# Start addresses of weight units against the activations in a float32r two-block network on one NeuronCore

## The chip, the cores and the metric

One of the eight cores of a Trainium2 chip runs the kernel. The metric is the device time of one execution in microseconds, the median over several runs. Engines are named as in the profile: PE is the matmul engine and PEld its weight loads, DVE, ACT and POOL are the vector, scalar and GpSimd engines, SP issues most of the transfers.

## The reference

Two small networks of depth 2 follow each other on 256 tokens of width 1024, batch 1. Everything is float32.

```python
# first block, for i in 0, 1
x = layer_norm(a * x + 0.5 * swiglu(x, w1[i,0], w3[i,0], w2[i,0]))
x = layer_norm(a * x + token_mixing(x, w_in[i], ...))    # RWKV-7, gated linear attention, gated delta rule
x = layer_norm(a * x + 0.5 * swiglu(x, w1[i,1], w3[i,1], w2[i,1]))
x = layer_norm(a * x + sigmoid(x @ ple_gate[i]) * (p[i] @ ple_proj[i]))
# second block, latent stream h and context stream hc of 256 tokens each
h, hc = x, ctx_2
# layer 0: attention over both streams, gated MLP on both; layer 1: HGRN2, MLP on h
```

The feed-forward width is 2816 (22 tiles of 128). Nearly all arithmetic is a product of 256 tokens with a large weight matrix.

## The kernel before

**Weight units.** All large weights lie in DRAM as units of 128 partitions by 1024 float32 (512 KB). `unit` (L67) fetches one: `split` (L71) has SP start the transfer into `wr` (L77), ACT rounds it to float32r into `wh` (L78), and DVE writes the rest, `wr - wh`, into `wl` (L79). There are four buffers each of `wr` and `wh` and three of `wl`. Activations are held in the same way as a high part `xh` and a low part `xl` (in the feed-forward's middle `hh` and `hl`, in the mixing branches `bh` and `bl`). A product of two such numbers is three matmuls: high by high, low weight by high, high weight by low.

**Feature-major products.** `fm` (L95) makes a result with features on the partitions. The weight tile of 128 columns is the stationary operand and the activations, 256 tokens, are the moving one: L102 (`wh`, `xh`), L103 (`wl`, `xh`), L105 (`wh`, `xl`; L109 where the low parts are late). Each matmul has 256 columns and a weight load of its own. The up projections of the feed-forwards (`ffn2`, L132), part of the token mixing (`fm_tile`, L1141) and of HGRN2 (L1742, L1748) go this way. A unit feeds 24 of these matmuls for one stream of tokens. `ffn2` takes a list of streams: in layer 0 of the second block it has two, and then both use a unit one after the other, all 48 matmuls of a pair of units for the first stream, then 48 for the second.

**Token-major products.** `tm2` (L163) makes a result with tokens on the partitions: the activations are stationary, and the weights move, 512 columns (256 where the last block is cut in two) per matmul: L178 (`xh`, `wh`), L179 (`xh`, `wl`), L180 (`xl`, `wh`). The down projections, the gates, the branch projections (`proj`, L1115) and the output projections go this way.

**Order.** Each engine runs its own instructions in program order; which instruction stands where comes from tables of numbers that place side work between weight units. PE has the weight load of the next matmul run beside the matmul before it.

**Addresses.** A pool lays its tiles one behind the other in each partition's bytes. In the built program of before, every `wh` and `wl` begins 32 bytes past a multiple of 128 (38560, 42656, ... ; 54944, ...), and so do the first stream's `xh` and `xl` (67232, 75424). The second stream's (108224, 116416) begin 64 past a multiple of 128; so do all `hh`, `hl`, `bh` and `bl`. A step of k moves the weights by 512 bytes and the activations by 1024, so these remainders hold for the whole tile. The *distance* of a matmul is below: start of its moving operand less start of the stationary operand that is loaded beside it (that of the next matmul), modulo 128.

Of the kernel before, what the change touches and what calls it, by code (L numbers as in the profile page):

```python
# [10 lines left out]
F32 = mybir.dt.float32  # L11
F32R = mybir.dt.float32r
# [5 lines left out]
P = 128  # L18
# [4 lines left out]
KF = 22  # L23
# [4 lines left out]


PIECES = (slice(0, 256), slice(256, 1024))  # L30


class Core:
# [30 lines left out]
        self.dr = E(tc.tile_pool(name="dr", bufs=1, space=bass.MemoryType.DRAM))  # L64


    def unit(self, src):  # L67
        self.tick()
        return self.split(src)

    def split(self, src):  # L71
        nc = self.nc
        hi = self.wh.tile([P, 1024], F32R, tag="wh", name=self.nm("wh"))
        lo = self.wl.tile([P, 1024], F32R, tag="wl", name=self.nm("wl"))
        raw = lo.bitcast(F32)
        raw = self.wr.tile([P, 1024], F32, tag="wr", name=self.nm("wr"))
        nc.sync.dma_start(raw, src)  # L77
        on_act = nc.scalar.copy(hi, raw)  # L78
        on_dve = nc.vector.tensor_tensor(lo, raw, hi.bitcast(F32), ALU.subtract)  # L79
        if self.queue:  # L80
            for op, first in zip((on_act, on_dve), self.queue.pop(0)):
                self.behind(op, first)
        return hi, lo
# [48 lines left out]
    def ffn2(self, up, down, xs, scale, sink, aside={}):  # L132


        nc = self.nc
        with self.tc.tile_pool(name=self.nm("hp"), bufs=1, reuse_waits="tile") as hp:
            hs = []
            for i in range(len(xs)):
                hs.append((hp.tile([P, KF, T], F32R, tag=f"hh{i}", name=self.nm("hh")),
                           hp.tile([P, KF, T], F32R, tag=f"hl{i}", name=self.nm("hl"))))  # L140
            for m in range(KF):
                if m == 3:
                    self.load_later()
                if m in aside:
                    aside[m]()
                w = [self.unit(up[2 * m]), self.unit(up[2 * m + 1])]
                for (xh, xl), (hh, hl) in zip(xs, hs):
                    pa, pv = self.acc(), self.acc()
                    self.fm([pa[:, :T], pv[:, :T]], w, xh, xl, late=m == 0)
                    th = hp.tile([P, T], F32, tag="th", bufs=3, name=self.nm("th"))  # L150
                    nc.scalar.activation(th, pa[:, :T], AF.Tanh, scale=0.5)  # L151
                    g = hp.tile([P, T], F32, tag="g", bufs=3, name=self.nm("g"))
                    nc.vector.scalar_tensor_tensor(g, th, 1.0, pa[:, :T], ALU.add, ALU.mult)
                    nc.vector.scalar_tensor_tensor(g, g, 0.5 * scale, pv[:, :T], ALU.mult, ALU.mult)  # L154
                    nc.scalar.copy(hh[:, m], g)  # L155
                    nc.vector.tensor_tensor(hl[:, m], g, hh[:, m].bitcast(F32), ALU.subtract)
            self.spot("down")
            self.tm2(down, 0, 2, hs, KF, sink, cut=True)

    def tm(self, src, b0, nblk, xh, xl, nk, sink, last=6, cut=False):  # L160
        self.tm2(src, b0, nblk, [(xh, xl)], nk, lambda n, i, t, ps, *c: sink(n, t, ps, *c), last, cut=cut)

    def tm2(self, src, b0, nblk, xs, nk, sink, last=6, lead=0, cut=False):  # L163

        nc = self.nc
        w = {}

        def mm(z, k, b, first, end):  # L170
            u = b // 2
            if u not in w:
                w[u] = self.unit(src[u])
            o, i, t, c = z
            h, l = (x[:, (b % 2) * 512 + c.start:(b % 2) * 512 + c.stop] for x in w[u])
            s = slice(t * P, t * P + P)
            xh, xl = xs[i]
            nc.tensor.matmul(o, xh[:, k, s], h, start=first, stop=False)  # L178
            nc.tensor.matmul(o, xh[:, k, s], l, start=False, stop=False)  # L179
            nc.tensor.matmul(o, xl[:, k, s], h, start=False, stop=end)  # L180

        self.load_later()
        for n in range(nblk):
            it = [(self.acc(), i, t, slice(0, 512)) for i in range(len(xs)) for t in range(2)]
            if cut and n == nblk - 1:
                o, i, t, _ = it.pop()
                it += [(o[:, :256], i, t, slice(0, 256)), (self.spare()[:, :256], i, t, slice(256, 512))]
            ahead = lead if n == 0 else 0
            tail = 0 if n < nblk - 1 else min(nk - ahead, last if len(xs) == 1 else last // 2)
            seq = [(k, z) for i in (1, 0) for k in range(ahead) for z in it if z[1] == i]  # L190
            seq += [(k, z) for k in range(ahead, nk - tail) for z in it]
            for k, z in seq:
                mm(z, k, b0 + n * nk + k, k == 0, k == nk - 1)
            for z in it:
                for k in range(nk - tail, nk):
                    mm(z, k, b0 + n * nk + k, k == 0, k == nk - 1)
                o, i, t, c = z
                sink(n, i, t, o, *((c,) if cut else ()))
# [198 lines left out]
class Mix(Core):  # L397
# [35 lines left out]
    def inv16(self, stg):  # L433

        nc = self.nc
        V = nc.vector
        sel = [self.cc("sel")[:, i:i + 1] for i in range(2)]
        fl = lambda z: z.rearrange("p a h u -> p a (h u)")
        at = self.t([P, 16, 32], "iA", bufs=2)
        V.transpose(at, fl(stg))  # L440
        a = self.t([P, 16, 16], "ia")
        V.tensor_scalar_mul(a, at[:, :, 0:16], sel[0])
        V.scalar_tensor_tensor(a, at[:, :, 16:], sel[1], a, ALU.mult, ALU.add)
        x = self.t([P, 16, 16], "ix")
        nc.gpsimd.memset(x, 0.0)
        nc.gpsimd.memset(x.rearrange("p a b -> p (a b)")[:, 0:256:17], 1.0)
        pr = self.t([P, 16, 16], "ip")
        for i in range(1, 16):
            V.tensor_tensor(pr[:, :i, :i], x[:, :i, :i], a[:, i, :i].rearrange("p (s o) -> p s o", o=1).broadcast_to([P, i, i]), ALU.mult)
            V.tensor_reduce(x[:, i, :i], pr[:, :i, :i].rearrange("p s c -> p c s"), mybir.AxisListType.X, ALU.add)  # L450
        e = self.t([P, 16, 32], "iA", bufs=2)
        for h in range(2):
            nc.scalar.activation(e[:, :, 16 * h:16 * h + 16], x.rearrange("p t s -> p s t"), AF.Identity, scale=sel[h])
        o = self.t([P, 16, 2, 16], "iB")
        V.transpose(fl(o), e)
        return o
# [626 lines left out]
class Block(Mix):  # L1083
# [15 lines left out]
    def proj(self, l, n, o):  # L1099

        nc = self.nc
        first = not self.merged
        bh = self.t([P, 4, T], "bh", F32R, pool=self.late)
        bl = self.t([P, 4, T], "bl", F32R, pool=self.late)
        self.to_fm(lambda t: o[:, t], bh, bl, nk=4)

        def sink(half, t, ps):
            g = self.gt[n, half]
            nc.vector.scalar_tensor_tensor(g[:, t], g[:, t], 1.0, ps, ALU.add, ALU.mult)
            if first:  # L1110
                self.merged[half] = g
            else:
                m = self.merged[half]
                nc.gpsimd.tensor_tensor(m[:, t], m[:, t], g[:, t], ALU.add)
        self.tm(self.a["wbr"][l, n], 0, 2, bh, bl, 4, sink)  # L1115

    def rw_tile(self, i, ps, st={}):
        nc = self.nc
# [21 lines left out]

    def fm_tile(self, i):  # L1141
        p = self.acc()[:, :T]
        self.fm([p], [self.unit(self.wfm[i])], self.xh, self.xl)
        return p

    def token_mix(self, l, pool, ln):
# [121 lines left out]
    def first(self, es, ep, stop=None):  # L1268
        nc, tc, a = self.nc, self.tc, self.a
# [6 lines left out]

        def last_pool():
            self.xq = es.enter_context(tc.tile_pool(name="xq", bufs=1, reuse_waits="tile"))
            return self.xq
        self.consts()  # L1280
        self.x_load(pool())
# [46 lines left out]
class Second(Block):  # L1328
# [371 lines left out]
    def hgrn(self, h, st, xs):  # L1700
        nc, tc, a = self.nc, self.tc, self.a
        V = nc.vector
        with tc.tile_pool(name="hg", bufs=1, reuse_waits="tile") as p:
# [9 lines left out]
            m = tl([P, KD], "lm")  # L1713
# [17 lines left out]
            xh, xl = (self.xp.tile([P, KD, T], F32R, tag=f"x{c}0", name=self.nm("xo")) for c in "hl")  # L1731
# [5 lines left out]
            def gates(j):  # L1737
# [1 line left out]

                z = tl([P, 4, T], "z", bufs=2)  # L1740
                for d in range(2):
                    w = self.unit(a["whfm"][3 * j + d])  # L1742
                    ps = self.acc()
                    for i in range(2):
                        self.fm([ps[:, i * T:i * T + T]], [w], *xs[i])
                    nc.scalar.activation(z[:, d:4:2], ps.rearrange("p (i t) -> p i t", i=2), AF.Tanh, scale=0.5)
                pq = self.acc()[:, :T]
                self.fm([pq], [self.unit(a["whfm"][3 * j + 2])], *xs[0])  # L1748
                q = tl([P, T], "hq", bufs=2)
                nc.scalar.copy(q, pq)  # L1750
                g = tl([P, 4, T], "hgl")
# [342 lines left out]
```

## Time and profile before

| | |
|---|---|
| median of 3 runs | 2857.93 us (2857.44 to 2858.2) |
| the profiled execution | 2860.42 us, span 2858.6 us |
| mean granted clock of PE | 0.984 |
| PE busy | 2763.0 us, 97% |
| DVE, ACT, POOL busy | 1890.3, 1300.3, 203.1 us |
| read from HBM | 420.36 MB |

The profile comes from one execution, which took 2.5 us more than the median. PE's busy time is a union of pipelined matmuls, each of which is recorded as longer than its distance to the next, so the pace of the matmuls is read from their starts and not from their durations.

### The profile page before, as it was taken

The numbers are of one execution on the slowest core, as the hardware profiler recorded it, in microseconds if no ns is written. First come the engines' busy times: TensorE is split into PE (matmuls) and PEld (weight loads), VectorE is DVE, ScalarE is ACT, GpSimd is POOL, SyncE is SP. The second block draws the span as 40 slices with busy tenths as digits, with TensorE's granted clock in tenths as the row PEclk, the third lists the DMA queues.
The fourth block names the chain that finished last, engine by engine and source line by source line (L and its number), as shares of the span: only waits on it lengthen the run. The fifth ranks groups of instructions, "written<-read, shape, count | busy, mean of one in ns | idle before, by whom it ended". The sixth has DMA issues, their size and how long they took to land.

```text
span 2858.6 us, 47580 instructions
## 1 busy us (share of the span) xinstructions
PE 2763.0 (97%) x18676; PEld 2443.4 (85%) x18676; DVE 1890.3 (66%) x3852; ACT 1300.3 (45%) x2040; POOL 203.1 (7%) x332
## 2 busy tenths in 40 slices
PE   9999999999999999999999998999999999999998
PEld 8978887669978987887778986798999888898897
DVE  5658885876556657876777656786444327799664
ACT  4436543535434435634444534564333226565543
POOL 0000211020000001211010001200000001000000
PEclk9999999999999999999999999999999999999999
DMA  7555333465566555423366556202322433224554
GB/s 253 184 195 171 119 121 104 142 238 180 185 210 213 183 180 189 129 99 118 118 224 223 179 174 224 81 31 76 102 89 90 129 99 111 75 65 153 181 182 150
DMA packets 117008, 426.63 MB, mean 149 GB/s; under 512 B 13600, under 2 KB 14112, under 8 KB 115760
## 3 DMA queue, kind: packets, MB, share of 16 engines
q1 hardware_dynamic: 115168, 419.01, 44.2%
q0 software_dynamic: 1472, 4.51, 0.5%
q8 instruction: 147, 2.41, 0.3%
q14 instruction: 77, 0.63, 0.1%
q10 hardware_dynamic: 144, 0.07, 0.0%
HBM read 420.36 MB, written 3.18 MB: 148 GB/s over the span
## 4 chain that ended last, share of the span: by engine, by line
PE 83%; DVE 10%; ACT 3%; DMA 2%; issue 2%; POOL 0%; DVEq 0%; POOLq 0%; SPq 0%; ACTq 0%
PE ps L102 13%; PE ps L103 13%; PE ps L105 12%; PE ps L179 10%; PE ps L180 10%; PE ps L178 10%; DVE wl L79 2%; PE pc L487 2%; PE pc L1649 1%; PE pc L1395 1%; PE pt L243 1%; PE pt L1633 1%; PE pt L1836 1%; ACT wh L78 1%; DMA modd<-row 1%
## 5 line engine op out<-in xcount | busy, mean ns | idle before, releaser
L79 DVE TENSOR_TENSOR wl<-wr,wh 128x1024 fp32r<-128x1024 f32 x658 | 812.2, 1236 | 557.7 <-issue 198.1
L78 ACT CAST wh<-wr 128x1024 fp32r<-128x1024 f32 x658 | 688.4, 1049 | 647.9 <-PE ps L180 293.7
L102 PE MATMUL ps<-xh,wh 128*128 128x256 f32 x3280 | 938.1, 287 | 10.0 <-ACT wh L78 4.0
L103 PE MATMUL ps<-xh,wl 128*128 128x256 f32 x3280 | 932.0, 285 | 2.2 <-DVE wl L79 2.1
L105 PE MATMUL ps<-xl,wh 128*128 128x256 f32 x3168 | 900.5, 285 | 0.4 <-DVE xl L254 0.3
L102 PEld LDWEIGHTS ps<-xh,wh 128*128 128x128 f32 x3280 | 632.8, 193 | 20.8 <-ACT wh L78 6.1
L103 PEld LDWEIGHTS ps<-xh,wl 128*128 128x128 f32 x3280 | 632.4, 193 | 8.8 <-issue 4.2
L105 PEld LDWEIGHTS ps<-xl,wh 128*128 128x128 f32 x3168 | 607.4, 192 | 5.0 <-issue 3.4
L178 PE MATMUL ps<-wh,xh 128*128 128x512 f32 (+1 forms) x624 | 245.0, 396 | 5.3 <-ACT wh L78 2.9
L179 PE MATMUL ps<-wl,xh 128*128 128x512 f32 (+1 forms) x624 | 246.5, 395 | 0.8 <-DVE wl L79 0.7
L180 PE MATMUL ps<-wh,xl 128*128 128x512 f32 (+1 forms) x624 | 244.1, 393 | 0.0
L180 PE MATMUL ps<-wh,hl 128*128 128x512 f32 (+1 forms) x616 | 228.4, 371 | 0.0
L179 PE MATMUL ps<-wl,hh 128*128 128x512 f32 (+1 forms) x616 | 228.1, 370 | 0.0
L178 PE MATMUL ps<-wh,hh 128*128 128x512 f32 (+1 forms) x616 | 227.6, 370 | 0.0
L178 PEld LDWEIGHTS ps<-wh,xh 128*128 128x128 f32 x624 | 118.1, 190 | 35.7 <-ACT wh L78 3.4
L179 PEld LDWEIGHTS ps<-wl,xh 128*128 128x128 f32 x624 | 118.5, 190 | 25.3 <-DVE wl L79 2.7
L180 PEld LDWEIGHTS ps<-wh,xl 128*128 128x128 f32 x624 | 118.7, 190 | 22.3 <-issue 0.7
L151 ACT ACTIVATE th<-ps 128x256 f32<-128x256 f32 x154 | 59.2, 384 | 170.7 <-PE ps L105 160.3
L178 PEld LDWEIGHTS ps<-wh,hh 128*128 128x128 f32 x616 | 115.9, 188 | 22.6 <-DVE g L154 0.4
L179 PEld LDWEIGHTS ps<-wl,hh 128*128 128x128 f32 x616 | 115.7, 188 | 21.9
L180 PEld LDWEIGHTS ps<-wh,hl 128*128 128x128 f32 x616 | 115.7, 188 | 21.4
L155 ACT CAST hh<-g 128x256 fp32r<-128x256 f32 x154 | 62.6, 406 | 116.7 <-DVE g L154 116.6
(566 smaller groups left out, 3718.4 us busy)
## 6 DMA issues: line engine op xcount, KB each, us to landing
wr<-in_up SPq DMA_DIRECT2D x264, 512.0 KB, 3.4
wr<-in_down SPq DMA_DIRECT2D x132, 512.0 KB, 3.3
wr<-in_wtm SPq DMA_DIRECT2D x72, 512.0 KB, 3.3
wr<-in_wfm SPq DMA_DIRECT2D x62, 512.0 KB, 3.6
fr<-in_ada SPq DMA_DIRECT2D x23, 1024.0 KB, 5.6
wr<-in_ada SPq DMA_DIRECT2D x38, 512.0 KB, 4.2
wr<-in_wbr SPq DMA_DIRECT2D x24, 512.0 KB, 4.0
wr<-in_whfm SPq DMA_DIRECT2D x24, 512.0 KB, 3.3
```

The costliest lines, as they stand in the source:

```text
L78: on_act = nc.scalar.copy(hi, raw)
L79: on_dve = nc.vector.tensor_tensor(lo, raw, hi.bitcast(F32), ALU.subtract)
L102: nc.tensor.matmul(o, hi[:, w], xh[:, k], start=k == 0, stop=False)
L103: nc.tensor.matmul(o, lo[:, w], xh[:, k], start=False, stop=False)
L105: nc.tensor.matmul(o, hi[:, w], xl[:, k], start=False, stop=k == nk - 1)
L151: nc.scalar.activation(th, pa[:, :T], AF.Tanh, scale=0.5)
L155: nc.scalar.copy(hh[:, m], g)
L178: nc.tensor.matmul(o, xh[:, k, s], h, start=first, stop=False)
L179: nc.tensor.matmul(o, xh[:, k, s], l, start=False, stop=False)
L180: nc.tensor.matmul(o, xl[:, k, s], h, start=False, stop=end)
L243: nc.tensor.transpose(pt[:, j, t * P:t * P + P], self.cols(src(t), t, k + j), self.ident)
L487: nc.tensor.matmul(ps[:, 64 * u:64 * u + 64], lhs[:, u], rhs[:, u], start=True, stop=True)
```

## The change

Tiles `wh` and `wl` become 128 bytes longer (1056 elements), and a unit takes 1024 elements of its tile from an offset that the caller gives: 16 elements (64 bytes) for feature-major products, 8 elements (32 bytes) for the branch projections and for the down projections of the first block, none for all other token-major ones. Since nothing else is free in a partition, the tile `iA` of the delta rule's inverse goes from two buffers to one; a filler of 96 bytes begins the pool `xq`, which holds the second stream.

```diff
+ROOM, FM_AT, HID_AT = 32, 16, 8
...
-    def unit(self, src):
+    def unit(self, src, at=0):
         self.tick()
-        return self.split(src)
-
-    def split(self, src):
+        return self.split(src, at)
+
+    def split(self, src, at):
         nc = self.nc
-        hi = self.wh.tile([P, 1024], F32R, tag="wh", name=self.nm("wh"))
-        lo = self.wl.tile([P, 1024], F32R, tag="wl", name=self.nm("wl"))
-        raw = lo.bitcast(F32)
+        hi = self.wh.tile([P, 1024 + ROOM], F32R, tag="wh", name=self.nm("wh"))[:, at:at + 1024]
+        lo = self.wl.tile([P, 1024 + ROOM], F32R, tag="wl", name=self.nm("wl"))[:, at:at + 1024]
...
-                w = [self.unit(up[2 * m]), self.unit(up[2 * m + 1])]
+                w = [self.unit(up[2 * m], FM_AT), self.unit(up[2 * m + 1], FM_AT)]
...
-            self.tm2(down, 0, 2, hs, KF, sink, cut=True)
+            self.tm2(down, 0, 2, hs, KF, sink, cut=True, at=0 if self.fr is None else HID_AT)
...
-                w[u] = self.unit(src[u])
+                w[u] = self.unit(src[u], at)
...
-        at = self.t([P, 16, 32], "iA", bufs=2)
+        at = self.t([P, 16, 32], "iA")
...
-        e = self.t([P, 16, 32], "iA", bufs=2)
+        e = self.t([P, 16, 32], "iA")
...
-        self.tm(self.a["wbr"][l, n], 0, 2, bh, bl, 4, sink)
+        self.tm(self.a["wbr"][l, n], 0, 2, bh, bl, 4, sink, at=HID_AT)
...
-        self.fm([p], [self.unit(self.wfm[i])], self.xh, self.xl)
+        self.fm([p], [self.unit(self.wfm[i], FM_AT)], self.xh, self.xl)
...
             self.xq = es.enter_context(tc.tile_pool(name="xq", bufs=1, reuse_waits="tile"))
+            self.xq.tile([P, 24], F32, name="fillq")
...
-                    w = self.unit(a["whfm"][3 * j + d])
+                    w = self.unit(a["whfm"][3 * j + d], FM_AT)
```

(`self.fr` is None only in the second block; `tm` hands `at` on to `tm2`; the second use of `whfm` changes in the same way.) No instruction is added or removed, and the order on every engine is the same as before; what changes are addresses, and with them some semaphore waits of POOL, DVE and SP on earlier users of the same bytes.

The distances in the two built programs, over all pairs of matmuls of these products that follow each other (a pair is counted under the moving operand of its first):

| product, columns | distance before | distance after | pairs |
|---|---|---|---|
| feature-major, 256 | 0 | 64 | 8237 |
| feature-major, 256 | 32 | 64 | 1428 |
| token-major, 512 | 0 | 0 | 1502 |
| token-major, 512 | 96 | 0 | 1865 |
| token-major, 512 | 96 | 32 | 198 |
| token-major, 256 | 0 | 0 | 237 |
| token-major, 256 | 96 | 0 | 697 |
| token-major, 256 | 96 | 32 | 132 |

The 45 pairs left out lie at the seams between two kinds of product, or keep 96.

## Rows read from the trace of the kernel before

**Rows 1.** The page, part 1: busy time of each engine.

```profile
PE 2763.0 (97%) x18676; PEld 2443.4 (85%) x18676; DVE 1890.3 (66%) x3852; ACT 1300.3 (45%) x2040; POOL 203.1 (7%) x332
```

**Rows 2.** The page, part 4: the chain that ended last, by line.

```profile
PE ps L102 13%; PE ps L103 13%; PE ps L105 12%; PE ps L179 10%; PE ps L180 10%; PE ps L178 10%; DVE wl L79 2%; PE pc L487 2%; PE pc L1649 1%; PE pc L1395 1%; PE pt L243 1%; PE pt L1633 1%; PE pt L1836 1%; ACT wh L78 1%; DMA modd<-row 1%
```

**Rows 3.** Waits of PE: us in total, times, longest.

```profile
PE ps L102 <- ACT wh L78: 4.0, 3, 2.1
```

**Rows 4.** Windows, a first-block up projection: PE, PEld, DVE, ACT, POOL, clock, DMA, GB/s.

```profile
888.46:1011.44 122.98, 122.98 (x1028) 122.98 (x1026) 76.56 (x109) 59.90 (x87) 0.00 (x0) 1.00 0.58 185
```

**Rows 5.** Timeline of PE, two streams on one pair of units: start us, us.

```profile
2055.97 0.28 PE L102 MATMUL ps<-xh,wh 128*128 128x256 f32 x1
...
2061.72 0.28 PE L102 MATMUL ps<-xh,wh 128*128 128x256 f32 x1
...
2067.38 0.28 PE L102 MATMUL ps<-xh,wh 128*128 128x256 f32 x1
```

**Rows 6.** Groups of PE, inside the first, then the second stretch of rows 5.

```profile
L103 PE MATMUL ps<-xh,wl 128*128 128x256 f32 x17 | 4.8, 283 | 0.0
...
L105 PE MATMUL ps<-xl,wh 128*128 128x256 f32 x17 | 4.8, 281 | 0.0
L103 PE MATMUL ps<-xh,wl 128*128 128x256 f32 x17 | 4.7, 278 | 0.0
L102 PE MATMUL ps<-xh,wh 128*128 128x256 f32 x16 | 4.5, 280 | 0.0
```

**Rows 7.** Timeline and windows of PE: a gate at distance 0, 87 matmuls apart.

```profile
413.73 0.39 PE L180 MATMUL ps<-wh,xl 128*128 128x512 f32 x1
...
433.47 0.39 PE L180 MATMUL ps<-wh,xl 128*128 128x512 f32 x1
...
413.74:433.46 19.72, 19.72 (x88) 16.32 (x87) 19.07 (x63) 9.93 (x12) 6.70 (x4) 1.00 0.59 180
```

**Rows 8.** The same of a down projection at distance 96, 135 matmuls apart.

```profile
138.96 0.40 PE L178 MATMUL ps<-wh,hh 128*128 128x512 f32 x1
...
170.46 0.28 PE L178 MATMUL ps<-wh,hh 128*128 128x256 f32 x1
...
139.00:170.45 31.45, 31.45 (x137) 25.32 (x136) 15.45 (x15) 12.51 (x13) 0.00 (x0) 1.00 0.59 192
```

**Rows 9.** Timeline of PE: 256 columns at distance 96, then 0; 35 matmuls apart.

```profile
1068.95 0.28 PE L178 MATMUL ps<-wh,hh 128*128 128x256 f32 x1
...
1073.10 0.28 PE L180 MATMUL pc<-wh,hl 128*128 128x256 f32 x1
...
1501.04 0.28 PE L178 MATMUL ps<-wh,xh 128*128 128x256 f32 x1
...
1505.23 0.28 PE L180 MATMUL pc<-wh,xl 128*128 128x256 f32 x1
```

**Rows 10.** Around a matmul with no weight load beside it: groups, then PEld's timeline.

```profile
L103 PE MATMUL ps<-xh,wl 128*128 128x256 f32 x1 | 0.3, 279 | 0.0
...
323.18 0.19 PEld L103 LDWEIGHTS ps<-xh,wl 128*128 128x128 f32 x1
325.89 0.30 PEld L487 LDWEIGHTS pc<-iz,NT 128*128 128x128 f32 x2 [2.52 <-issue]
```

**Rows 11.** Timeline of PE: eight transposes; groups: one transpose's length.

```profile
603.83 1.03 PE L243 MATMUL pt<-cst,gate 128*128 128x128 f32 x8
...
L1420 PE MATMUL pt<-cst,row 128*128 128x128 f32 x1 | 0.3, 272 | 0.0
```

**Rows 12.** Groups of DVE and ACT in the stretch of rows 4; windows: the first 100 us.

```profile
L79 DVE TENSOR_TENSOR wl<-wr,wh 128x1024 fp32r<-128x1024 f32 x44 | 53.9, 1225 | 36.0 <-issue 27.6 <-PE ps L103 8.0 <-ACT wh L78 0.5
L78 ACT CAST wh<-wr 128x1024 fp32r<-128x1024 f32 x44 | 46.0, 1048 | 31.9 <-issue 28.8 <-PE ps L105 3.1
...
0.00:100.00 100.00, 92.88 (x748) 91.79 (x749) 59.99 (x90) 49.14 (x74) 1.28 (x12) 1.00 0.69 234
```

More of the change, by code (lines that the diff above doesn't have):

```diff
@@ L157, in ffn2, with tm, tm2 @@
             self.spot("down")
-            self.tm2(down, 0, 2, hs, KF, sink, cut=True)
-    def tm(self, src, b0, nblk, xh, xl, nk, sink, last=6, cut=False):
-        self.tm2(src, b0, nblk, [(xh, xl)], nk, lambda n, i, t, ps, *c: sink(n, t, ps, *c), last, cut=cut)
-    def tm2(self, src, b0, nblk, xs, nk, sink, last=6, lead=0, cut=False):
+            self.tm2(down, 0, 2, hs, KF, sink, cut=True, at=0 if self.fr is None else HID_AT)
+    def tm(self, src, b0, nblk, xh, xl, nk, sink, last=6, cut=False, at=0):
+        self.tm2(src, b0, nblk, [(xh, xl)], nk, lambda n, i, t, ps, *c: sink(n, t, ps, *c), last, cut=cut, at=at)
+    def tm2(self, src, b0, nblk, xs, nk, sink, last=6, lead=0, cut=False, at=0):
         nc = self.nc
@@ L1747, in gates @@
                 pq = self.acc()[:, :T]
-                self.fm([pq], [self.unit(a["whfm"][3 * j + 2])], *xs[0])
+                self.fm([pq], [self.unit(a["whfm"][3 * j + 2], FM_AT)], *xs[0])
                 q = tl([P, T], "hq", bufs=2)
```

## The prediction

> **What bounds the kernel now.** I read part 1 of the page first. PE is busy 97% of the span [rows 1]. Durations of pipelined matmuls overlap, so that alone proves little; the next two views do. In the chain that ended last, the feature-major lines L102, L103 and L105 hold 38% of the span, the token-major lines L178 to L180 hold 30%, and DVE's best line 2% [rows 2]. Of PE's waits for weights the largest is 4.0 us in total [rows 3]. So two thirds of the time is matmuls of weight units, one behind the other, and what counts is their pace, start to start. In a first-block up projection 1028 matmuls of 256 columns take 122.98 us, at a granted clock of 1.00, while SP moves 185 GB/s [rows 4]: about 120 ns each, and nobody is waited for. A change of one nanosecond in that pace is worth about 9 us over the kernel.
>
> The view that bears on the change is one that the kernel holds by accident. In layer 0 of the second block two streams use the same pair of units one after the other, and only the second stream's address differs: the first is at distance 0, the second at distance 32. The first stream's 48 matmuls run from 2055.97 to 2061.72, the second's 48 from 2061.72 to 2067.38 [rows 5]. That is 5.75 / 48 = 119.8 ns against 5.66 / 48 = 117.9 ns, with the same weights, instructions and clock. Inside the two stretches one L103 matmul is 283 ns long in the first and 278 in the second, L105 281 and L102 280 [rows 6]. The distance matters, and distance 0, which 8237 of 9665 feature-major pairs have, is the worse of the two.
>
> In the token-major products the sign is the other way. At distance 0 a gate's matmuls of 512 columns run from 413.73 to 433.47, 87 steps: 226.9 ns [rows 7]. At distance 96 a down projection's run from 138.96 to 170.46, 135 steps: 233.3 ns [rows 8]. The lengths are 0.39 and 0.40 us in the same rows. Both stretches have clock 1.00, and DVE is the busier in the faster one, so its traffic is not the reason.
>
> **Feature-major units to distance 64.** No row shows 256 moving columns at distance 64, so I bound the pace. From above: nothing gained is 119.8 [rows 5], and the worst that a distance does in the trace is the 6.4 ns between rows 7 and 8, which would make 126.2. From below: eight transposes, each with a weight load of 128 columns and half as many moving columns, take 1.03 us [rows 11], and the last is about 0.27 long, so (1.03 - 0.27) / 7 = 109 ns: a weight load per matmul can't go faster than that here. Between these ends two rows point to the same place. First, 32 bytes took off 1.9 ns, and 64 is the farthest point of a circle of 128: the same again gives 116.0. Second, a matmul that has no other weight load beside it (its own starts at 323.18, the next at 325.89) is 279 ns long [rows 10], 4 ns shorter than the 283 at distance 0 [rows 6]; 119.8 - 4 = 115.8. If the loss comes from the load beside the matmul, a good distance can take off about that much. I take 116.0. The sum: 8237 x 3.8 ns = 31.3 us, and the 1428 pairs that stand at 32 now, 1428 x 1.9 = 2.7; together 34.0. Not all of it lies on the path: the three lines hold 38% of 2858.6 = 1086 us of the chain [rows 2], while 8237 x 119.8 + 1428 x 117.9 ns = 1155 us, a share of 0.94. That leaves **32.0 us**.
>
> [...]
>
> **Token-major units to distance 0.** 1865 pairs of 512 columns go from 96 to 0: 1865 x (233.3 - 226.9) = 11.9 us. 697 pairs of 256 columns make the same step, and there it costs: 35 steps take 1073.10 - 1068.95 = 4.15 us at 96, 118.6 ns, and 1505.23 - 1501.04 = 4.19 us at 0, 119.7 ns [rows 9]; 697 x 1.1 = 0.8 us lost. On the chain lie 30%, 858 us, of 1502 x 226.9 + 2063 x 233.3 + 1066 x 119 ns = 949 us, a share of 0.90: 11.1 x 0.90 = **10.0 us**. The 198 pairs of 512 columns that land at 32 I leave as they are; between 0's pace and as much again on the other side they are worth 1.3 us either way.
>
> **The rest.** No instruction is added and the order stays. Each unit's consumer gets faster, so the supply must hold: a unit serves 24 matmuls, 2.88 us now and 2.78 after, and asks 1.23 us of DVE and 1.05 of ACT [rows 12]; DVE is busy 76.56 of 122.98 us in that stretch [rows 4], which leaves a third free. The transfers go from 185 to about 191 GB/s, and the first 100 us already run at 234 with the same pace [rows 12]. Without this cover the supply would end a unit, not the matmuls, and the gain would stop there. The single buffer of `iA` adds no wait to ACT or DVE; the moved waits on POOL and SP name users of the bytes that finished stages earlier. I cost them at nothing. Should one be real, it lengthens the mixing's chain by one short memset.
>
> **The sum.** 32.0 + 10.0 = 42.0 us off the profiled execution's 2860.4 gives 2818.4. The median of the runs stands 2.5 us lower, 2857.9, so I forecast **2816**.
>
> **Rivals.**
> *The gain stops at 32 bytes.* If any distance but 0 is as good as another, the pace at 64 is 117.9: 8237 x 1.9 x 0.94 = 14.7, and with the 10.0 it makes 2833. For it: at 256 columns, 96 [rows 9] is not better than 32. Against it: the bare matmul of rows 10 is shorter than the mean of the three in the second stretch of rows 6 by a little only, 279 to 279.7, so it can't be excluded. Chance 0.23.
> *More of the loss goes.* At the lower bound of 109 the kernel would come to 2857.9 - 10.0 - (8237 x 10.8 + 1428 x 8.9) x 0.94 ns = 2752; halfway between that and 116, at 112.5, to 2784. Against it: the bare matmul [rows 10] shows no such room. Chance 0.18, of which 0.10 at 2784 or above.
> *64 is the same as 0.* If the addresses repeat every 64 bytes, the main part gains nothing and the second stream loses its 1.9 ns: 10.0 - 1428 x 1.9 x 0.94 ns = 7.4 us, 2850.5. Nothing in the rows excludes it. Chance 0.07, split 0.04 and 0.03 over the bound below.
> *The addresses do nothing.* Were the two streams of rows 5 different for a reason of their own, the change would not do what it says, and the time stays at 2857.9. [...] The trace disagrees, 119.8 against 117.9 ns with the weights shared [rows 5]. Chance 0.04.
> *Slower.* In rows 7 and 8 leaving distance 0 costs 6.4 ns per matmul. If the feature-major matmuls react like these at 64, their moving reads being held up by the load beside them, they go to 126.2: (8237 x 6.4 + 1428 x 8.3) x 0.94 = 60.7 us lost, 10.0 gained, 2908.6. It decides from a pace of 120.6 upwards (9665 x 0.94 pairs times 1.1 ns eat the 10.0). Against it: at 32 the same product moved down. Chance 0.07.
>
> **How the numbers follow.** The forecast (a pace of 115 to 117, 2807 to 2825) has 0.41. A measurement of this kernel can tell about 0.2%, 5.7 us, from no change. Faster: 0.41 + 0.23 + 0.18 + 0.04 = 0.86; within: 0.03 + 0.04 = 0.07; slower: 0.07. The range takes in the forecast, the stop at 32, the upper part of the larger gain and the wrap at 64: 2782 to 2851. Left out are 0.08 + 0.04 + 0.07 = 0.19.
>
> **What would show it.** In the profile after, an up projection of 1028 matmuls should take about 119 us, not 123, with PE still at full clock and without waits for weights; the two streams of the second block should show the same pace, near 116, and L102's mean length should fall from 283 to about 279. A down projection of the first block should step by 227 ns, not 233. If the two streams come out equal at 118, the gain stops at 32; if the up projection stays at 120 while the down projection moves, it is the wrap; if L79 or L78 end PE's waits in the up projections, the supply took the gain.

## The result and the profile after

The changed kernel takes **2820.04 us** (median of 4 runs, 2817.08 to 2826.01); the kernel before, run beside it, 2857.68 (2856.82 to 2858.2). The ratio is 0.987, 95% interval [0.9858, 0.9883]: 37.6 us faster, inside the forecast range, 4 us above the forecast of 2816. The profiled execution after took 2826.01 us, span 2824.2, which is 34.4 less than the profiled execution before.

The page after, its parts 1, 4 and 5 (in 5: busy us, mean ns of one, then idle time before them):

```profile
PE 2723.2 (96%) x18676; PEld 2403.6 (85%) x18676; DVE 1891.3 (67%) x3852; ACT 1299.3 (46%) x2040; POOL 201.6 (7%) x332
...
PE ps L105 12%; PE ps L106 12%; PE ps L108 12%; PE ps L182 10%; PE ps L181 10%; PE ps L183 10%; DVE wl L82 2%; PE pc L490 2%; PE pc L1653 1%; PE pc L1399 1%; PE pt L246 1%; PE pt L1637 1%; ACT wh L81 1%; PE pt L1840 1%; PE pc L661 1%
...
L105 PE MATMUL ps<-xh,wh 128*128 128x256 f32 x3280 | 924.1, 283 | 11.7 <-ACT xh L250 5.9
L106 PE MATMUL ps<-xh,wl 128*128 128x256 f32 x3280 | 918.3, 281 | 3.3 <-DVE wl L82 3.3
```

Lines stand three further down than before: L105, L106, L108 are the feature-major matmuls, L181 to L183 the token-major ones, L82 the rest `wl`. DVE, ACT and POOL are as busy as before to within 1.5 us, PE 39.8 us less [rows 1]. No engine took PE's place in the chain; the feature-major lines hold 36% instead of 38% [rows 2].

Windows of after: the up projection of [rows 4], the first block's second down projection, the gate of [rows 7], the up projection with two streams, and the mixing of layer 1 (PE, PEld, DVE, ACT, POOL, clock, DMA, GB/s):

```profile
871.45:987.63 116.18, 116.18 (x1027) 116.18 (x1026) 76.70 (x109) 60.21 (x87) 0.00 (x0) 1.00 0.63 196
752.99:784.18 31.19, 31.19 (x137) 25.34 (x136) 15.40 (x15) 12.45 (x13) 0.00 (x0) 1.00 0.59 193
407.73:427.84 20.11, 20.11 (x88) 16.33 (x87) 19.47 (x63) 9.90 (x12) 7.10 (x4) 1.00 0.59 183
1977.34:2213.38 236.04, 236.04 (x2033) 236.04 (x2033) 103.94 (x174) 76.12 (x129) 1.67 (x1) 1.00 0.31 101
1060.50:1496.60 436.10, 414.59 (x2542) 338.06 (x2542) 330.03 (x857) 205.84 (x356) 57.42 (x96) 0.95 0.43 146
```

Between the starts at 871.44 and 987.63 lie 1025 steps of the up projection, 116.19 us / 1025 = 113.4 ns each; before they were 120.0. The second down projection, 135 steps, stands at 231.2 ns; before, all four of the first block stood at 233.3, the first of them in [rows 8]. The gate, which was at distance 0 before and should have stayed there, takes 20.11 us instead of 19.72 [rows 7]: 231.4 ns a step instead of 226.9. The same two-stream stretch as [rows 5], PE's timeline after:

```profile
2035.08 0.28 PE L105 MATMUL ps<-xh,wh 128*128 128x256 f32 x1
...
2040.73 0.28 PE L105 MATMUL ps<-xh,wh 128*128 128x256 f32 x1
...
2046.20 0.28 PE L105 MATMUL ps<-xh,wh 128*128 128x256 f32 x1
```

48 matmuls take 5.65 us, then 5.47: 117.7 and 114.0 ns. Other pairs of stretches there give 115.9 and 118.3; the mean of the whole up projection is 236.05 / 2032 = 116.2.

By stage, between the same matmuls of both profiled executions, this is where the 34.4 us come from:

| stages | before, us | after, us | difference | the changed kernel profiled again |
|---|---|---|---|---|
| up projections, six stages (one of them with two streams) | 912.3 | 874.8 | -37.5 | -38.5 |
| down projections, six stages | 454.5 | 450.4 | -4.1 | -4.1 |
| mixing of layer 1 | 428.2 | 436.2 | +7.9 | +1.4 |
| all the rest | 1063.6 | 1062.8 | -0.8 | -0.6 |

Of the 4.1 us of the down projections 2.2 lie between the first and the last matmul of each; the rest lies in the normalisation behind the first and the third.

The mixing of layer 1 needs a word, for 6.5 of its 7.9 us did not come again in the second profile. The same stretch in the profile of before, and in a second profile of the changed kernel, has 0.97 where the first profile of after has 0.95. Windows, of before:

```profile
1085.00:1513.30 428.30, 409.43 (x2543) 334.79 (x2543) 329.97 (x858) 206.23 (x356) 57.44 (x96) 0.97 0.45 149
```

and of the changed kernel's second profile:

```profile
1057.93:1487.54 429.61, 408.80 (x2543) 332.86 (x2543) 330.33 (x858) 206.12 (x356) 57.57 (x96) 0.97 0.42 149
```

The instructions are the same, and so are the busy times of DVE, ACT and POOL; 6.5 us lie between two executions of one kernel, and the longer one has the lower clock, 0.95 against 0.97 in the mean. Below this stretch takes 440.0 us in one kernel, at 0.94, and 425.5 in another, at 0.97, so a few microseconds between two medians are read with that in mind.

### The profile page after: what moved, and what is told of

The parts are those of the page before. It is cut to its first block, busy times and chain, and to the rows that moved or that the text cites. A ratio compares the mean times of both kernels' runs of the same rounds, so it can differ in the third digit from the quotient of the medians.

```text
span 2824.2 us, 47580 instructions
## 1 busy us (share of the span) xinstructions
PE 2723.2 (96%) x18676; PEld 2403.6 (85%) x18676; DVE 1891.3 (67%) x3852; ACT 1299.3 (46%) x2040; POOL 201.6 (7%) x332
## 4 chain that ended last, share of the span: by engine, by line
PE 82%; DVE 11%; ACT 3%; DMA 2%; issue 2%; POOL 0%; DVEq 0%; POOLq 0%; SPq 0%; ACTq 0%
PE ps L105 12%; PE ps L106 12%; PE ps L108 12%; PE ps L182 10%; PE ps L181 10%; PE ps L183 10%; DVE wl L82 2%; PE pc L490 2%; PE pc L1653 1%; PE pc L1399 1%; PE pt L246 1%; PE pt L1637 1%; ACT wh L81 1%; PE pt L1840 1%; PE pc L661 1%
## 5 line engine op out<-in xcount | busy, mean ns | idle before, releaser
L82 DVE TENSOR_TENSOR wl<-wr,wh 128x1024 fp32r<-128x1024 f32 x658 | 813.1, 1238 | 524.0 <-issue 184.3
L105 PE MATMUL ps<-xh,wh 128*128 128x256 f32 x3280 | 924.1, 283 | 11.7 <-ACT xh L250 5.9
L106 PE MATMUL ps<-xh,wl 128*128 128x256 f32 x3280 | 918.3, 281 | 3.3 <-DVE wl L82 3.3
L108 PE MATMUL ps<-xl,wh 128*128 128x256 f32 x3168 | 885.4, 280 | 0.1
L105 PEld LDWEIGHTS ps<-xh,wh 128*128 128x128 f32 x3280 | 624.4, 190 | 23.7 <-ACT xh L250 7.1
L106 PEld LDWEIGHTS ps<-xh,wl 128*128 128x128 f32 x3280 | 623.1, 190 | 9.6 <-DVE wl L82 4.4
L108 PEld LDWEIGHTS ps<-xl,wh 128*128 128x128 f32 x3168 | 598.5, 189 | 5.2 <-issue 4.1
L181 PE MATMUL ps<-wh,xh 128*128 128x512 f32 (+1 forms) x624 | 246.7, 398 | 5.2 <-ACT wh L81 3.0
L183 PE MATMUL ps<-wh,xl 128*128 128x512 f32 (+1 forms) x624 | 245.6, 395 | 0.0
L181 PE MATMUL ps<-wh,hh 128*128 128x512 f32 (+1 forms) x616 | 227.7, 370 | 0.1
L183 PE MATMUL ps<-wh,hl 128*128 128x512 f32 (+1 forms) x616 | 227.2, 369 | 0.0
L182 PE MATMUL ps<-wl,hh 128*128 128x512 f32 (+1 forms) x616 | 226.9, 368 | 0.0
L181 PEld LDWEIGHTS ps<-wh,xh 128*128 128x128 f32 x624 | 118.4, 190 | 36.6 <-ACT wh L81 3.5
L182 PEld LDWEIGHTS ps<-wl,xh 128*128 128x128 f32 x624 | 119.6, 192 | 26.1 <-DVE wl L82 2.1
L183 PEld LDWEIGHTS ps<-wh,xl 128*128 128x128 f32 x624 | 119.1, 191 | 23.8 <-issue 0.7
L181 PEld LDWEIGHTS ps<-wh,hh 128*128 128x128 f32 x616 | 115.7, 188 | 21.6 <-DVE g L157 0.5
L183 PEld LDWEIGHTS ps<-wh,hl 128*128 128x128 f32 x616 | 115.6, 188 | 21.1
```

What stands on the lines that cost most here:

```text
L105: nc.tensor.matmul(o, hi[:, w], xh[:, k], start=k == 0, stop=False)
L106: nc.tensor.matmul(o, lo[:, w], xh[:, k], start=False, stop=False)
L108: nc.tensor.matmul(o, hi[:, w], xl[:, k], start=False, stop=k == nk - 1)
```

## The experiments

**A finer distance.** Each tile is now 4224 bytes long, which is 16 times 256 plus 128. So neighbouring buffers of `wh` begin at 160 and 32 past a multiple of 256 by turns; before, all began at 160. Modulo 128, as the change counts, nothing shows of this; modulo 256 the distances of after are 64 and 192 by turns in the feature-major products, 0 and 128 by turns in most token-major ones. From here on *distance* is modulo 256 (what is 96 modulo 128 in the kernel before is 224). The theory: the circle is 256 bytes long, and the alternation cost the token-major products what they should have gained. Its rival: the gate's 4.5 ns come from something else that the change moved, the single buffer of `iA` or the place of the activations.

**1. Longer tiles without offsets** (the single `iA` and the filler stay).

```diff
-ROOM, FM_AT, HID_AT = 32, 16, 8
+ROOM, FM_AT, HID_AT = 32, 0, 0
```

> The changed kernel with longer weight tiles, filler and single iA, but no offsets (64 and 32 bytes go to 0). If the gain comes from the distance of 64 in the feature-major products, it is gone: these go back to 119.8 ns a matmul, 2855 to 2870 us. If it came from the layout or the moved waits, most of it stays, 2820 to 2835. Second question: the tiles now step by 4224 bytes, so the remainder of 256 alternates between buffers. If only the remainder of 128 counts, the gates at distance 0 keep 226.9 ns as before the change; if the remainder of 256 counts, they go to 231 as after it (about 6 us more than before, 2864).

Measured: 2853.65 us (10 runs) against 2859.97 (13 runs), ratio 0.9979 [0.9969, 0.9989]. Windows, an up projection and the gate:

```profile
883.39:1005.33 121.94, 121.94 (x1027) 121.94 (x1026) 76.73 (x109) 60.14 (x87) 0.00 (x0) 1.00 0.58 187
412.09:432.18 20.09, 20.09 (x88) 16.34 (x87) 19.45 (x63) 9.92 (x12) 7.09 (x4) 1.00 0.56 182
```

The time is 6 us below the kernel before and just under the range of 2855 to 2870, because the up projections moved a little too: at 0 and 128 by turns they step by 119.0 ns, one below 120.0. The gate, whose units start at the same offset in their tiles as before, stands at 20.09 us already. So the gain of the change needs the 64 bytes, and the gate loses its pace without them, by the longer tiles or by `iA` and the filler; run 3 tells which.

**2. The feature-major offset alone.**

```diff
-ROOM, FM_AT, HID_AT = 32, 16, 8
+ROOM, FM_AT, HID_AT = 32, 16, 0
```

> The changed kernel with the 64 bytes of the feature-major units alone; the down projections and branch projections go back to distance 96. If the token-major part gave nothing in the end, the time is that of the change, 2818 to 2826; if it gave the 10 us that were forecast, 2830.

Measured: 2824.7 us (2821.51 to 2834.52, 4 runs), 0.9885 [0.9864, 0.9905], beside 0.987 [0.9858, 0.9883] for the whole change. The up projections of one stream stand at 113.4 ns, the first three down projections at 233.6. Nearly all of the gain is here; what the token-major offsets add can't be told from nothing by these intervals.

**3. Tiles that step by a multiple of 256.** `ROOM` 64 makes a tile 4352 bytes long; a table is loaded in two halves to make room for it (the same in 4, 5 and 8 to 12).

```diff
-ROOM, FM_AT, HID_AT = 32, 16, 8
+ROOM, FM_AT, HID_AT = 64, 16, 8
...
-                lf = p2.tile([P, 7 * P], F32, name="lvf2")
-                nc.sync.dma_start(lf, a["lvm"][:, 448:])
-                nc.gpsimd.tensor_copy(lvm, lf)
+                for z in range(2):
+                    lf = p2.tile([P, 448], F32, name=f"lvf{2 + z}", tag="lvf")
+                    nc.sync.dma_start(lf, a["lvm"][:, 448 + 448 * z:896 + 448 * z])
+                    nc.gpsimd.tensor_copy(lvm[:, 448 * z:448 * z + 448], lf)
```

> The changed kernel with 256 instead of 128 bytes of room per weight tile, so tiles step by 4352 bytes and every buffer has the same remainder of 256 (a small table is loaded in two halves to make space). If the alternating remainder of 256 is what keeps token-major matmuls at 231 ns, those at distance 0 go back to 226.9 and the kernel gains 5 to 8 us: 2810 to 2816. If only the remainder of 128 counts, nothing changes: 2818 to 2824, gates at 231 ns.

Measured: 2826.38 us (2818.25 to 2843.52, 4 runs), 0.9892 [0.9855, 0.993]. Windows: the first up projection, the third, the second down projection:

```profile
14.53:137.13 122.60, 122.60 (x1043) 122.60 (x1042) 77.47 (x112) 60.04 (x89) 0.56 (x1) 1.00 0.64 211
890.14:1006.31 116.17, 116.17 (x1027) 116.17 (x1026) 76.71 (x109) 60.15 (x87) 0.00 (x0) 1.00 0.63 196
772.09:802.70 30.61, 30.61 (x137) 25.35 (x136) 15.38 (x15) 12.46 (x13) 0.00 (x0) 1.00 0.60 194
```

The down projection at distance 0 takes 30.61 us, 226.8 ns a step; where this kernel has 128, a step is 232.3 to 232.4. For the token-major products the circle is 256, and the rival falls: `iA` and the activations' place are as in the change. But the time did not follow (2810 to 2816 was expected): the first up projection stands at 117.8 ns, the third at 113.4, and both are at distance 192 throughout. Neither theory has a place for that.

**4 and 8. Two sweeps.** The first four feed-forwards get offsets of their own, in run 4 as below, in run 8 (40, 48, 56, 16); one run each. `unit` in the up projections takes `up_at`, `tm2` in the down projections `down_at`.

```diff
+FFN_AT = list((0, 8, 24, 32)) + [None] * 2
...
+        z = FFN_AT[self.ffns]
+        self.ffns += 1
+        up_at, down_at = (z, z) if z is not None else (FM_AT, 0)
...
```

> As e3, but the four feed-forwards of the first block begin their units at 0, 32, 96 and 128 bytes: up projections at distances 0, 224, 160 and 128 of 256. One theory, the circle of 128: 0 and 128 give 119.8 ns, 224 and 160 give about 118. The other, the circle of 256: 128 is the farthest point and gives 113 or less, 160 lies between. The down projections stand at 224, 0, 64 and 128: by the circle of 128, 233, 227, unknown and 227 ns.

> As e4 with offsets of 160, 192, 224 and 64 bytes: up projections at distances 96, 64, 32 and 192 of 256. Taken with e4, the circle of 256 gives 118 to 118.5 ns at 96 and 32, 117.8 at 64 and 113.3 at 192. Were it the circle of 128, 64 and 192 would be alike. The down projections stand at 128, 160, 192 and 160; by e3 and e4 232 ns at 128 and 234 at 160.

Measured: 2832.96 and 2842.11 us (one run each). Paces by distance, in ns a step, one or two stages each, from stages of 1024 steps (feature-major; two pieces of 460 and 285 at 128) or 135 steps (token-major; the value at 32 is run 7's):

| distance | 0 | 32 | 64 | 96 | 128 | 160 | 192 | 224 |
|---|---|---|---|---|---|---|---|---|
| feature-major, 256 columns | 120.0 | 116.7 | 113.3 | 120.0 | 118.7 | 118.7 | 113.3 or 117.8 | 118.3 |
| token-major, 512 columns | 227.0 | 233.3 | 229.0 | - | 232.5 | 234.3 | 233.3 | 233.3 |

The circle of 128 is excluded for both kinds: 0 and 128 differ by 1.3 ns in the feature-major row, where every one-stream up projection of the kernel before stands at 120.0 and all five pieces of the stage at 128 at 118.6 or 118.7, and by 5.5 ns in the other row. But what the expectations took from a circle of 256 missed as well: 128, its farthest point, was to give 113 or less and gave 118.7; 96, 64 and 32 were to give 118 to 118.5, 117.8 and again 118 to 118.5, and gave 120.0, 113.3 and 116.7. So the table is a finding and no theory's. (In the built programs the fourth down projection stands at 0 in run 4 and at 192 in run 8, not at 128 and 160 as expected.) Rows of run 4 (windows: up projections at 224 and 160, down projections at 64 and, the fourth, at 0):

```profile
643.22:764.50 121.28, 121.28 (x1028) 121.28 (x1026) 76.72 (x109) 60.16 (x87) 0.00 (x0) 1.00 0.60 188
881.32:1002.96 121.64, 121.64 (x1028) 121.64 (x1027) 76.66 (x109) 59.93 (x87) 0.00 (x0) 1.00 0.58 187
1003.09:1033.76 30.67, 30.67 (x136) 25.17 (x135) 15.19 (x15) 12.22 (x13) 0.00 (x0) 1.00 0.59 194
1634.05:1664.43 30.38, 30.38 (x137) 25.15 (x135) 15.17 (x15) 12.24 (x13) 0.00 (x0) 1.00 0.60 196
```

and three of run 8 (windows: up projections at 96, 64 and 32):

```profile
15.02:139.68 124.66, 124.66 (x1040) 124.66 (x1040) 76.79 (x110) 59.77 (x88) 0.56 (x1) 1.00 0.58 206
642.05:758.21 116.16, 116.16 (x1027) 116.16 (x1026) 76.72 (x109) 60.13 (x87) 0.00 (x0) 1.00 0.58 196
878.31:997.89 119.58, 119.58 (x1027) 119.58 (x1026) 76.77 (x109) 60.32 (x87) 0.00 (x0) 1.00 0.56 191
```

And its fourth up projection, at 192 throughout, has both paces one behind the other. Windows of the two long pieces of that stage, 460 and 285 steps of 117.8 and 113.4 ns:

```profile
1511.05:1565.20 54.15, 54.15 (x461) 54.15 (x461) 35.35 (x53) 27.93 (x43) 2.35 (x4) 1.00 0.54 189
1600.04:1632.32 32.28, 32.28 (x287) 32.28 (x286) 22.20 (x34) 17.36 (x26) 0.00 (x0) 1.00 0.55 190
```

PE's timeline where the first piece ends (start, us):

```profile
1565.33 0.28 PE L109 MATMUL ps<-xl,wh 128*128 128x256 f32 x1
1565.45 0.60 PE L250 MATMUL pt<-cst,pj 128*128 128x128 f32 x4
1565.81 0.36 PE L106 MATMUL ps<-xh,wh 128*128 128x256 f32 x1
```

Four transposes stand between; behind them the next 93 steps go at 113.6 ns, and the pace then stays. So at this distance there are two paces, a sequence kept the one it began with, and the pace changed at a break. The clock is 1.00 in both pieces, the traffic 189 and 190 GB/s.

**5. All feature-major units at 192, all token-major ones at 0,** on top of run 3.

```diff
...
-            self.tm2(down, 0, 2, hs, KF, sink, cut=True, at=0 if self.fr is None else HID_AT)
+            self.tm2(down, 0, 2, hs, KF, sink, cut=True, at=HID_AT if self.ffns < 4 else 0)
...
-            self.xq.tile([P, 24], F32, name="fillq")
+            self.xq.tile([P, 56], F32, name="fillq")
```

> As e3, with the second stream's filler 128 bytes longer and the down projections of the last three feed-forwards from offset 0, so that every feature-major pair stands at 192 of 256 and every token-major one (but 23) at 0. If the remainder of 256 sets the pace, feature-major matmuls go at 113.3 ns (117.8 in a stage that falls into the other pattern) and token-major ones at 226.9 everywhere: against the changed kernel 3200 pairs of 512 columns at 4 ns less and the two-stream projection at 113.3, some 10 to 18 us: 2803 to 2813 where the changed kernel has 2820. If only the remainder of 128 counts, it is the changed kernel again.

Measured: 2823.51 us (2823.12 to 2827.9, 4 runs), 0.9891 [0.9876, 0.9906]. The 2803 to 2813 were missed. Windows, the third up projection, the one with two streams, and the mixing of layer 1:

```profile
869.79:985.95 116.16, 116.16 (x1027) 116.16 (x1026) 76.43 (x109) 59.67 (x87) 0.00 (x0) 1.00 0.57 196
1973.69:2213.00 239.31, 239.31 (x2033) 239.31 (x2033) 103.99 (x174) 76.17 (x129) 1.75 (x1) 1.00 0.29 100
1058.39:1498.40 440.01, 420.20 (x2542) 345.27 (x2542) 330.29 (x858) 206.54 (x356) 57.52 (x96) 0.94 0.41 146
```

Every down projection of the first block stands at 226.8 ns as intended, but the two-stream stage and the last up projection took the slower of the two paces, 117.7 to 117.8, and the mixing of layer 1 was long again, 440.0 us at a clock of 0.94.

**6. The changed kernel again,** beside 5 and 7, without an edit.

> The changed kernel beside e5 on one chip: 2817 to 2826 us, 0.987 of the kernel before. The up projections at 113.4 ns, the gates at 231.

Measured: 2821.07 us (2818.62 to 2821.61, 4 runs), 0.988 [0.9863, 0.9896]; up projections at 113.3 to 113.7 ns in their long stretches, the two-stream one at 116.2, the gate at 231.3, as in the first profile. With units at 64 and 192 by turns the long stretches of one stream did not take the slower pace in either profile; three stretches of 95 steps in the fourth up projection lie between, at 114.4 to 116.7.

**7. The activations moved, not the weights.** The kernel before, with one buffer of `iA`, the halved table and a filler ahead of the activations:

```diff
...
+        self.xp.tile([P, 48], F32, name="fillx")
...
```

> The kernel before with weight tiles and units as they were, and the activations moved instead: a filler of 192 bytes ahead of the first stream (a single iA buffer and the halved table make room). The feature-major pairs stand at 192 of 256, the second stream at 224, the gates at 64, the down and branch projections at 32. If the distance counts and not where the weights begin, up projections go at 113.3 ns, gates near 229, and the time is 2808 to 2822. If the place or length of the weight tiles is what helped, up projections stay at 119.8 and the time at 2855 to 2865.

Measured: 2821.03 us (2818.88 to 2839.43, 4 runs), 0.9893 [0.9861, 0.9925]. Windows, the second and the third up projection, both at 192:

```profile
639.45:755.62 116.17, 116.17 (x1027) 116.17 (x1026) 76.74 (x109) 60.32 (x87) 0.00 (x0) 1.00 0.60 196
874.32:995.03 120.71, 120.71 (x1027) 120.71 (x1026) 76.72 (x109) 60.29 (x87) 0.00 (x0) 1.00 0.54 189
```

The weights lie where they lay before, in tiles of the old length, and the gain is the same (the changed kernel beside it took 2821.07 us): what counted here is the distance, not where a unit begins or how long its tile is. Both paces appear again, 113.3 and 117.8 ns, here in two stages with the same addresses of weights and activations.

**9. Alternate on purpose.** Since units at 64 and 192 by turns kept the better pace in 6, kernel 5 gets them by turns too, with the token-major units all at 0.

```diff
...
+        fm, n, self.units2 = at == FM_AT, self.units2, self.units2 + 1
+        ah, al = (16 + 32 * (n % 2), 16 + 32 * (n % 3 == 1)) if fm else (at, at)
-        hi = self.wh.tile([P, 1024 + ROOM], F32R, tag="wh", name=self.nm("wh"))[:, at:at + 1024]
-        lo = self.wl.tile([P, 1024 + ROOM], F32R, tag="wl", name=self.nm("wl"))[:, at:at + 1024]
+        hi = self.wh.tile([P, 1024 + ROOM], F32R, tag="wh", name=self.nm("wh"))[:, ah:ah + 1024]
+        lo = self.wl.tile([P, 1024 + ROOM], F32R, tag="wl", name=self.nm("wl"))[:, al:al + 1024]
```

> As e5, but feature-major units begin by turns at 64 and 192 bytes, with the same turns as the changed kernel's buffers have (wh every second, wl every third unit). If the turns are what keeps the changed kernel's feature-major matmuls out of the 117.8 ns pattern, single-stream up projections go at 113.3 to 113.7 in every stage and the two-stream one at 116.2, with the token-major ones at 226.9 as in e5: 2808 to 2816, unless the mixing loses clock. If the pattern is drawn by chance at a stage's begin, some up projection shows 117.8 again.

Measured: **2801.68 us** (2795.65 to 2804.93, 5 runs) against 2857.66 (9 runs), ratio **0.9808 [0.9791, 0.9825]**: faster than the kernel before, and by the ratios faster than the changed one, whose interval ends at 0.9858. It is also below the 2808 to 2816 expected, chiefly because the two-stream stage gained where 116.2 ns was expected to stay. Windows: the third up projection, the one with two streams, the third down projection, the mixing of layer 1:

```profile
870.41:986.63 116.22, 116.22 (x1027) 116.22 (x1026) 76.77 (x109) 60.00 (x87) 0.00 (x0) 1.00 0.61 196
1960.78:2191.14 230.36, 230.36 (x2033) 230.36 (x2033) 103.95 (x174) 76.12 (x129) 1.60 (x1) 1.00 0.32 104
986.75:1017.37 30.62, 30.62 (x137) 25.34 (x136) 15.40 (x15) 12.46 (x13) 0.00 (x0) 1.00 0.60 197
1059.04:1484.55 425.51, 405.41 (x2543) 331.84 (x2543) 330.27 (x858) 206.29 (x356) 57.45 (x96) 0.97 0.45 150
```

All long stages stand at 113.3 to 113.5 ns, with two streams too (230.36 us against 236.04 after the change), and the down projection at 226.8. The shorter sequences in HGRN2, 119 steps each, lie between, at 115.3 to 116.9. The mixing of layer 1, at the same clock of 0.97 as before the change, is 2.8 us shorter.

**10, 11 and 12. Which half stands where.** Kernel 9 with a fixed rule: `wh` begins 64 bytes into its tile and `wl` 192, as below; in run 11 the reverse, (48, 16). These are offsets. An offset of 64 is the distance 192, as in run 5, and an offset of 192 the distance 64: in runs 10 and 12 the high halves stand at distance 192 and the low ones at 64, the other way round than run 12's text puts it.

```diff
-        ah, al = (16 + 32 * (n % 2), 16 + 32 * (n % 3 == 1)) if fm else (at, at)
+        ah, al = (16, 48) if fm else (at, at)
```

> As e5, with wh at 64 bytes and wl at 192: distances 64 on L102's pairs and 192 on the two others. If each pair's own distance sets its pace, a mean between 113.3 and 117.8; if the three lock as a whole, one of the two values in every stage.

> The reverse of e10: wh at 192 bytes and wl at 64, distances 192 on L102's pairs and 64 on the two others. The same question; a stage that holds 113.3 here and 117.8 in e10 would say which of the three matters.

> The high halves of every weight at 64 bytes from the activations and the low halves at 192, of a circle of 256; token-major units at 0. If the one look at this version tells its time, every feature-major stage stands at 113.3 to 113.5 ns a step, the two-stream up projection among them, the down projections at 226.8, and the median is 2800 to 2806 us, 0.981 of the kernel before. Rival: the better of the two paces is drawn anew in each run, as it was when all units stood at 192: then some stage stands at 117.8 or 118.9 ns in the profile, and the runs spread over 2800 to 2825 us.

Measured: run 10 2804.33 us, run 11 2820.3 (one run each); run 12, the kernel of 10 timed, 2803.12 (2795.42 to 2816.87, 5 runs), 0.9825 [0.9801, 0.985]. Windows, the two-stream stage of run 12:

```profile
1957.59:2187.97 230.38, 230.38 (x2033) 230.38 (x2033) 103.92 (x174) 76.22 (x129) 1.65 (x1) 1.00 0.31 104
```

the mixing of layer 1 of run 12:

```profile
1056.86:1483.33 426.47, 405.08 (x2542) 331.04 (x2543) 330.04 (x858) 206.37 (x356) 57.46 (x96) 0.97 0.43 151
```

and the second and third up projections of run 11:

```profile
633.53:749.70 116.17, 116.17 (x1027) 116.17 (x1026) 76.75 (x109) 60.14 (x87) 0.00 (x0) 1.00 0.62 196
868.14:989.98 121.84, 121.84 (x1027) 121.84 (x1026) 76.74 (x109) 60.01 (x87) 0.00 (x0) 1.00 0.58 187
```

With the high halves at distance 192 every long stage of both profiles stands at 113.3 to 113.5, and HGRN2 at 113.4 too. With the high halves at 64 there are two paces again: 113.4 in the first, the second and most of the fourth up projection, 118.9 in the third, the two-stream one, HGRN2 and the last.

Run 12's profile is that of its fastest execution, and the five spread over 21 us. The granted clocks on record account for that. Time times mean clock, an estimate of the time at full clock, is 2795.42 x 0.986 = 2756 us for the fastest and 2816.87 x 0.978 = 2755 for the slowest, and 2754 to 2756 for all five; one long stage at the slower pace would add 1024 x 4.4 ns = 4.5 us. (The third place of a clock is worth 1.4 us.) For run 9 it is 2756 to 2758. For run 5, with all units at 192, it goes from 2753 to 2770, and the profiled execution with its slow stages is the second highest, 2769. That fits a pace drawn anew in each execution; but the kernel before, too, ranges over 12 us in its largest set of runs, so it is not shown.

## Why the prediction was right, and where it was not

**The bound: right.** The pace of the weight units' matmuls set the time, and the distance set the pace; run 7 shows it with the weights left where they were, 113.3 and 117.8 ns instead of 120.0. Supply held: DVE still takes 76.70 us of the up projection's 116.18, at 196 GB/s, and `wl` ends only 3.3 us of L106's waits.

**Feature-major units to distance 64: right in kind, the pace too high.** I took 116.0 ns, the second of two equal steps around a circle of 128. Single streams stand at 113.3 to 113.8 in all long stretches; L105 is 276 ns long inside the up projection, 279 in the two-stream stage, not 283 [rows 6]. Over the whole trace, steps that follow each other directly have a mean of 114.7 after and 119.5 before. The up projections alone gave 37.5 us, where the sum had 6336 x 3.8 + 1056 x 1.9 ns = 26.1 for them. The bare matmul of [rows 10], 279 ns, was a poor bound: the mean of a matmul beside a load was 276 in that up projection.

**The share of 0.94: not the error.** Outside the feed-forwards the feature-major steps fell from 119.2 to 116.1 ns, some 7 us in all, and the steps of 512 columns rose from 230.0 to 231.2, 2.4 us. That leaves some 4 us to gain there; the stages outside came out 0.8 us longer in the second profile and 7.2 longer in the first, whose mixing of layer 1 ran at 0.95. It does not follow that such gains are lost as a rule: in runs 9 and 12, with that mixing at 0.97 as before, the steps outside the up and down projections sum to 11.1 and 13.4 us less, and the time outside them is 9.8 and 13.6 us shorter. Over the whole second profile 41.8 us arrive of 44.8 that the steps sum to, a share of 0.93.

**Token-major units to distance 0: this step failed.** It was to give 10.0 us. The pairs that came from 96 went from 233.3 to 231.2, not 226.9, and the pairs that stood at 0 already went from 226.9 to 231.4. Over all 512-column steps the mean stayed at 231.1 ns. What failed is the assumption that a remainder of 128 says it all: with buffers 4224 bytes apart, half of the pairs stand at 128 of 256. Run 1 shows the loss without any offset, run 3 the 226.8 ns once the step is a multiple of 256. What the down projections gained, 2.2 us between their first and last matmuls, the other token-major products lost.

**The two errors cancelled, and the close number is luck.** Mean steps times their number, from the traces of before and after (an estimate): feature-major 45.1 us gained where 34.0 was forecast before the share, token-major 0.5 us lost where 11.1 was to be gained. The sums are 44.6 measured and 45.1 forecast. The cause was right in kind for one term, too small by a third, and the other term did not come.

**The rivals.** *The gain stops at 32* would have left the up projections at 117.9: excluded by 113.4. *More of the loss goes* was nearer for the pace of the up projections, though its 112.5 for all gives 2784 by the same sum. *64 the same as 0* and *slower* are excluded by runs 1 and 2. *The addresses do nothing* is excluded by runs 1, 2 and 7: run 2 differs from run 1 in the 64 bytes alone, and the up projections stand at 113.4 instead of 119.0. Over all the distances tried the pace of a feature-major stage lies between 113.3 and 120.0 ns. The 109 ns a step that I took for the lower bound, an estimate from the transposes of [rows 11], was not reached: the best of any long stage here is 113.3.

## What to carry to other kernels

Where float32r matmuls each bring a weight load of their own, read the step between starts, stage by stage, and compare the start addresses of the moving operand and of the stationary one loaded beside it modulo 256, for every buffer of a pool: a tile whose length is no multiple of 256 (4224 bytes here) changes the distance from buffer to buffer. Of the distances tried here 0 was the best when the weights move in 512 columns (226.8 ns), 64 and 192 when 256 columns of activations do (113.3 ns; at 192 some stages had 117.8). For the latter, units placed at both by turns (run 9), or the high halves at distance 192 and the low ones at 64 (runs 10 and 12), held the better pace, 113.3 to 113.5 ns, in every long stage that was profiled; the reverse (run 11) had 118.9 in some. Compare the granted clock before you compare the times of a stage with gaps in PE's work: the mixing of layer 1 differed by 6.5 us between two executions of the changed kernel, at clocks of 0.95 and 0.97, and by 1.4 us between the kernels before and after, both at 0.97.

## What was not expected of the hardware

- The distance worked modulo 256 here (0 and 128 differ by 1.3 and 5.5 ns) and not evenly: 32 bytes from 96 to 64 are worth 6.7 ns of 120.0, and 0 is the best place for one kind of product and among the worst for the other (the table of the sweeps).
- One distance has two paces. At 192, stages of the same shape stand at 113.3 or 117.8 ns, in run 7 both at a clock of 1.00, with 196 and 189 GB/s; a stage kept its pace for a thousand matmuls, and one changed it at a break of four transposes. A mixture of 64 and 192 has 113.4 and 118.9 (run 11). What sets the choice at a sequence's start stays open; that no break may fall, or that another matmul might be put in to force the better one, wasn't tried.
- Which stationary operand counts isn't shown. The distance is taken to the one that is loaded beside the matmul; in all these runs the matmul's own stationary operand stands at the same distances, or in the same mixture.
- The pace of a mixture need not be the mean: at 0 and 128 by turns the first block's first three down projections stand at 231.2 to 231.4 ns after the change and the last of the kernel at 229.6, where the mean of 226.8 and 232.4 is 229.6; and distance 32, 116.7 ns in a stage of its own, is 117.9 between stretches at 0 [rows 5].
- Several paces lie at nearly equal steps: 113.3, 116.7 and 120.0 ns are 3.4 and 3.3 apart, 226.8 and 233.3 about twice that, 6.5. Others, 117.8, 118.3 and 118.7 ns, don't fit such steps. Nothing here shows why.
